# The opening of a one-core decoder layer: dummy products, meta tokens by two transposes, x in halves

## The chip, the core and the metric

The kernel runs on one core of a Trainium2 chip. The metric is the device time of one execution in microseconds (us), and the median of three runs is given. The core has a matrix engine (PE in the profile, with its weight loads as PEld), a vector engine (DVE), a scalar engine (ACT), GpSimd (POOL) and a sync engine (SP). SP, ACT and POOL also issue DMA transfers, each in the order of its own instruction stream.

## What is computed

One layer of a hybrid decoder trunk. 16 learned meta tokens stand ahead of 256 tokens of x, so 272 tokens of width 2048 go through. All values are float32.

```python
h = jnp.concatenate([meta_b, x], axis=1)          # 16 + 256 tokens, 2048 wide
u = rms_norm(h, g_pre_mix)
z_pool, v_conv, g_conv, gate_a, gate_b = jnp.split(u @ w_in, splits, axis=-1)
y_a = causal_multiscale_pool(z_pool, w_pool_grp, pool_scale) @ w_pool_out
y_b = conformer_conv(v_conv, g_conv, w_dw, ...) @ w_conv_out
m = sigmoid(gate_a) * y_a + sigmoid(gate_b) * y_b
h = h + rms_norm(m @ w_o, g_post_mix)
h = h + rms_norm(jnp.square(relu(rms_norm(h, g_pre_mlp) @ w_up)) @ w_down, g_post_mlp)
return h[:, 16:]
```

For this change only the first product counts: the columns `v_conv` of `u @ w_in`, and what has to be there before it can begin.

## The kernel before, in words

**Number format.** Each float32 operand is split into a rounded high part (`hi`, by a copy on ACT) and the rest (`lo`, by a subtraction on DVE). A product of two such operands is three passes on PE: high weight with high activation, high weight with low activation, low weight with high activation (`mm3`, line 417; its matmul is line 422). The activations are transposed so that channels lie on the 128 partitions: `u[:, k, 0, :]` is the high part and `u[:, k, 1, :]` the low part of channel group k (16 groups of 128), the first 16 columns being the meta tokens and the other 256 those of x. The norm's root is left out at first: only its gain `g_pre_mix` is multiplied in, and the root of each token is multiplied into the results later (`scale_roots`, `scale_rows`).

**Loads of the opening** (lines 323 to 334). SP loads `m_in`, the meta tokens as 16 rows of 2048 (128 KB). ACT loads the gain as 16 rows of 128 (`load_rows`, line 300). x comes in four blocks of 512 columns (`load_x`, line 318); block 0 goes as two transfers of 256 KB, one of its two token tiles on SP and one on ACT. `open_chunk` (line 233) begins a chunk of weights: it takes a buffer `raw` and issues its transfers; a chunk of the first stretch has eight row groups of 128 by 256 columns, which come in pieces of 1, 1, 2, 2 and 2 row groups on the queues that the argument `first` lists. x block 1 follows on ACT, block 2 on SP, then the second chunk, then block 3. POOL loads the small vectors and the taps. The transfers of SP and ACT count up eight semaphores in turn; a transfer that takes a semaphore for a second time waits, on the engine that issues it, until the transfer that had it before has landed. `warm_up(AF.Sqrt)` makes ACT load its function table.

**First work on PE.** `keep_warm(n)` (line 341) puts n transposes of the identity into a tile that nobody reads. Eight of them stand first. `meta_tokens` (line 351) then transposes `m_in` in 16 pieces of 16 rows by 128 columns (line 355), turns the gain into columns (`rows_to_columns`, lines 312 and 313), multiplies the two on DVE (`mg`, line 359), and splits the result into the first 16 columns of `u` (lines 360 and 361). Four more dummies follow.

**The first product** (lines 521 to 539). Two accumulators of 128 by 272 take 16 steps k. `x_tile(k)` (line 366) transposes the two token tiles of channel group k on PE (line 370) into a PSUM tile `xt`, from which ACT writes the high part (line 371) and DVE the low part (line 372). `pieces_to(n)` splits the weights' row groups up to n (lines 250 and 253). The loop runs four steps ahead of the product (`LEAD`): for k = -4 to -1 it only makes x tiles 0 to 3 and splits row groups 0 to 4. Then step k of the product is six matmuls of 272 columns, two times the three passes, and after each odd k two more x tiles are made. So x tiles 4 and 5, the first that need x block 1, stand behind the steps 0 and 1. Everything on an engine runs in the order in which it is written here; only later parts of the kernel are ordered by the planner at the top of the file (`Plan`).

Of the kernel before, what the change touches and what calls it, by code (L numbers as in the profile page):

```python
# [8 lines left out]
F32 = mybir.dt.float32  # L9
F32R = mybir.dt.float32r  # L10
AF = mybir.ActivationFunctionType
# [3 lines left out]
P = 128  # L15
CK = 4
CW = 512
# [83 lines left out]
def hybrid_block(ctx: ExitStack, tc: tile.TileContext, ins: dict, out: bass.AP):  # L101
    nc = tc.nc
    x = ins["x"][0]
    meta = ins["meta"]
    T, D = x.shape
    M = meta.shape[0]
    L = M + T
    NT = T // P
    KD = D // P
# [17 lines left out]
    const = ctx.enter_context(tc.tile_pool(name="const", bufs=1))  # L127
# [3 lines left out]
    tmp = ctx.enter_context(tc.tile_pool(name="tmp", bufs=2))  # L131
# [3 lines left out]
    def f32(ap):  # L135
        return ap.bitcast(F32)

    def acc_tile(name):
        return psA.tile([P, CW], F32, tag="acc", name=name)

    def misc_tile(name):
        return psB.tile([P, CW], F32, tag="misc", name=name)
# [43 lines left out]
    HALF = (2 * CK, CW // 2)  # L186
# [24 lines left out]
    opened = []  # L211
# [13 lines left out]
    def part_tile(tag, n, standing=False):  # L225

        key = f"{tag}{n % 3}"
        room = ready.pop(key) if key in ready else part_room(key, f"{tag}_{n}")
        place = 2 if standing and tag == "hi" else 1
        shift = (place - 1 - 3 * KEYS.index(key)) % 4 * LINE  # L230
        return room[:, shift:shift + CK * CW]

    def open_chunk(first=((2, nc.sync),) * 4):
        n = at["n"]
        at["n"] += 1
        src, (rows, width) = stream[n]
        raw = raws.tile([P, CK * CW], F32, tag="raw", name=f"raw_{n}")
        hi, lo = (part_tile(tag, at["parts"], n in standing_chunks) for tag in ("hi", "lo"))
        at["parts"] += 1
        flat, (raw, hi, lo) = raw, (t.rearrange("p (k c) -> p k c", k=rows) for t in (raw, hi, lo))  # L240
        pieces = rows if n < FIRST + 1 else 1
        k = rows // pieces
        i = 0
        for n_, queue in first if n < FIRST else ((rows, nc.sync),):
            sl = slice(i, i + n_)
            queue.dma_start(raw[:, sl, :], src[:, sl, :])
            i += n_

        def high(sl):
            nc.scalar.copy(hi[:, sl, :], raw[:, sl, :])  # L250

        def low(sl):
            nc.vector.tensor_sub(lo[:, sl, :], raw[:, sl, :], f32(hi[:, sl, :]))  # L253

        def piece(i):
            def f():
                sl = slice(i * k, (i + 1) * k)
                high(sl)
                low(sl)
            return f  # L260
        opened.append((hi, lo, [piece(i) for i in range(pieces)], flat))
# [13 lines left out]
        return opened.pop(0)[:2]  # L275


    ident = const.tile([P, P], F32, name="ident")
    make_identity(nc, ident)
    ones = const.tile([P, P], F32, name="ones")  # L280
# [3 lines left out]
    def warm_up(func):  # L284

        nc.scalar.activation(warm, ones[:, 0:1], func)
# [3 lines left out]
    m_in = big.tile([M, D], F32, tag="a", name="m_in")  # L290
# [9 lines left out]
    def load_rows(queue, *names):  # L300
        rows = tmp.tile([48, P], F32, tag="g", name=f"rows_{names[0]}")
        n = 0
        for name in names:
            v = ins[name][0].rearrange("(k p) -> k p", p=P)
            queue.dma_start(rows[n:n + v.shape[0], :], v)
            n += v.shape[0]
        return rows, n, names[0]

    def rows_to_columns(rows, n, name):

        pv = misc_tile(f"pv_{name}")
        nc.tensor.transpose(pv[:, :n], rows[:n, :], ident[:n, :n])
        nc.vector.tensor_copy(vecs[:, cols[name]:cols[name] + n], pv[:, :n])

    def col(name, k):
        return vecs[:, cols[name] + k:cols[name] + k + 1]

    def load_x(queue, b, ts=slice(0, NT)):
        sl = slice(b * CW, (b + 1) * CW)
        queue.dma_start(x_in[:, ts, sl], xv[:, ts, sl])  # L320


    nc.sync.dma_start(m_in, meta)
    pre_rows = load_rows(nc.scalar, "g_pre_mix")
    for t, queue in enumerate((nc.sync, nc.scalar)):
        load_x(queue, 0, slice(t, t + 1))
    open_chunk(((1, nc.scalar), (1, nc.sync), (2, nc.sync), (2, nc.sync), (2, nc.sync)))
    load_x(nc.scalar, 1)
    load_x(nc.sync, 2)
    open_chunk()  # L330
    load_x(nc.sync, 3)
    other_rows = load_rows(nc.gpsimd, "pool_scale", "b_dw", "conv_ln_g", "conv_ln_b", "g_pre_mlp")
    taps_in = big.tile([TAPS, CC], F32, tag="c", name="taps_in")
    nc.gpsimd.dma_start(taps_in, w_dw)
    ssq = const.tile([P, NT + 1, XB], F32, name="ssq")
    nc.gpsimd.memset(ssq, 1.0)
    warm_up(AF.Sqrt)

    idle = misc_tile("idle")

    def keep_warm(n):
        for _ in range(n):
            nc.tensor.transpose(idle[:, :P], ident, ident)

    keep_warm(8)

    u = big.tile([P, KD, 2, -(-L // (4 * LINE)) * 4 * LINE], F32R, tag="um", name="u")[:, :, :, :L]

    def meta_tokens():

        pt = acc_tile("xm")[:, :KD * M].rearrange("p (k m) -> p k m", k=KD)
        for k in range(KD):
            nc.tensor.transpose(pt[:, k, :], m_in[:, k * P:(k + 1) * P], ident[:M, :M])
        rows_to_columns(*pre_rows)
        mg = tmp.tile([P, KD, M], F32, tag="v", bufs=5, name="mg")
        g = vecs[:, cols["g_pre_mix"]:cols["g_pre_mix"] + KD]
        nc.vector.tensor_mul(mg, pt, g[:, :, None].broadcast_to([P, KD, M]))
        nc.scalar.copy(u[:, :, 0, :M], mg)  # L360
        nc.vector.tensor_sub(u[:, :, 1, :M], mg, f32(u[:, :, 0, :M]))

    meta_tokens()
    keep_warm(4)

    def x_tile(k):
        pt = acc_tile(f"xt_{k}")[:, :T]
        sl = slice(k * P, (k + 1) * P)
        for t in range(NT):
            nc.tensor.transpose(pt[:, t * P:(t + 1) * P], x_in[:, t, sl], ident)  # L370
        nc.scalar.activation(u[:, k, 0, M:], pt, AF.Copy, scale=col("g_pre_mix", k))
        nc.vector.scalar_tensor_tensor(
            u[:, k, 1, M:], pt, col("g_pre_mix", k), f32(u[:, k, 0, M:]),
            op0=ALU.mult, op1=ALU.subtract)

    def sq_tile(b, t):
        sl = slice(b * CW, (b + 1) * CW)
        junk = tmp.tile([P, CW], F32, tag="junk", bufs=1, name=f"sqx_{b}_{t}")
        src, n = (x_in[:, t, sl], P) if t < NT else (m_in[:, sl], M)
        nc.scalar.activation(junk[:n, :], src, AF.Square, accum_out=ssq[:n, t, b:b + 1])  # L380
# [6 lines left out]
        nc.vector.tensor_scalar(q, q, -0.5, 1.5, op0=ALU.mult, op1=ALU.add)  # L387
        nc.vector.tensor_mul(r, r, q)

    rb = const.tile([P, L], F32, name="rb")  # L390
    sc = {}

    def scale_roots():
# [23 lines left out]
    def mm3(acc, hi, lo, act, k, cs, first, last):  # L417


        off = act.shape[3] - acc.shape[1]  # L420
        for n, (w, a) in enumerate(((hi, 0), (hi, 1), (lo, 0))):
            nc.tensor.matmul(acc, w[:, k[0], cs], act[:, k[1], a, off:],  # L422
                             start=first and n == 0, stop=last and n == 2)
# [18 lines left out]
    def acc_tiles(name, n=CW // P):  # L442
        return [acc_tile(f"acc_{name}_{j}") for j in range(n)]
# [68 lines left out]
    def pieces_to(n):  # L512

        while first["split"] < min(n, (FIRST + 1) * HALF[0]):
            c = first["split"] // HALF[0]
            if c == at["n"]:
                open_chunk()
            opened[c][2].pop(0)()
            first["split"] += 1

    first = {"split": 0}
    accs = [acc[:, :L] for acc in acc_tiles("v0", HALF_CW // P)]
    squares = [(b, t) for b in range(XB) for t in range(NT + 1)]
    LEAD = 4
    for k in range(-LEAD, KD):
        if k < 0:
            x_tile(k + LEAD)

        pieces_to(min(k + LEAD + 1, KD) + 2 * max(k - KD + LEAD + 1, 0))
        if k < 0:  # L530
            continue
        if k >= HALF[0] and k % 2:
            sq_tile(*squares.pop(0))
        for j, acc in enumerate(accs):
            mm3(acc, *opened[k // HALF[0]][:2], u, (k % HALF[0], k), slice(j * P, (j + 1) * P),
                k == 0, k == KD - 1)
        if k % 2:
            for kx in range(k + LEAD - 1, min(k + LEAD + 1, KD)):
                x_tile(kx)
# [183 lines left out]
    for g in range(NG):  # L723
        for j in range(GK):
            q = g * GK + j
            acc = (acc_tile if q < KP - 2 else misc_tile)(f"acc_grp_{q}")[:, :T]
# [48 lines left out]
    for n in range(NB):  # L775
# [4 lines left out]
    m = big.tile([P, LINE + KD * 2 * T], F32R, tag="um", name="m")[:, LINE:].rearrange(  # L780
        "p (k a t) -> p k a t", k=KD, a=2)
# [421 lines left out]
    accs = acc_tiles("up00")  # L1203
# [498 lines left out]
    for e, cs in enumerate(col_halves):  # L1702
        for w, s in ends:
            h = AT[s][0]
# [47 lines left out]
```

## Time and profile before

| | |
|---|---|
| median of 3 runs | 1208.1 us (1207.75 to 1208.54) |
| the profiled execution's own time | 1208.15 us |
| its span in the profile | 1206.4 us |
| PE busy | 1195.8 us, 99% of the span |
| DVE busy | 974.7 us, 81% |
| ACT busy | 627.6 us, 52% |
| DMA | 238.27 MB, mean 198 GB/s |
| first dummy on PE | 1.35 us after the span's start |
| `m_in` needed and there | 3.87 us |
| first matmul of the first product | 8.26 us |
| x tile 4 on PE | 10.88 us |

Times in a view are microseconds from the start of the span. The profiled execution has 1.75 us outside the span. A row of the timeline is a run of equal instructions that follow one another on one engine: when the first began, how long it took until the last ended, and how many. The chain of waits is followed back from the last instruction of the window to what released it. A row of DMA issues gives the size of a transfer and the time from its issue to the landing of its last part; `ACTq` and `SPq` are the issuing streams of ACT and SP.

### The profile page before, as it was taken

What the parts mean: (1) busy time and instruction counts of PE and PEld (TensorE: products, weight loads), DVE (VectorE), ACT (ScalarE), POOL (GpSimd) and SP (SyncE); (2) the same over time, 40 slices, a digit from 0 to 9 for tenths busy, and PEclk for the clock granted to TensorE, in tenths of its full rate; (3) what the DMA queues carried; (4) which work ended last, traced back from release to release, by engine and by line L of the source; (5) the groups of instructions that cost most, each with busy time, mean ns of one, the idle gap of its engine ahead of it and who ended that gap; (6) DMA issues with size and microseconds to landing.
All of it is one profiled execution on the core that took longest, in us unless ns stands there. A gap on an engine that the chain in (4) does not pass through costs nothing.

```text
span 1206.4 us, 15712 instructions
## 1 busy us (share of the span) xinstructions
PE 1195.8 (99%) x6444; PEld 1038.4 (86%) x6444; DVE 974.7 (81%) x1058; ACT 627.6 (52%) x651; POOL 8.3 (1%) x19
## 2 busy tenths in 40 slices
PE   9999999999999999999999999999999999999997
PEld 9999988888888888898888888888888888888886
DVE  6799978999776778688988878778878778888756
ACT  7533344443583454665555564564554555555542
POOL 1000000000000000000000000000000000000000
PEclk9999999999999999999999999999999999999999
DMA  9655555656558578546475674674764764755841
GB/s 289 210 175 175 178 202 180 208 177 207 175 169 280 176 256 262 181 160 221 144 244 174 187 232 158 198 249 141 245 199 156 261 200 149 244 175 178 275 141 70
DMA packets 162038, 238.27 MB, mean 198 GB/s; under 512 B 4033, under 2 KB 91521, under 8 KB 161440
## 3 DMA queue, kind: packets, MB, share of 16 engines
q1 hardware_dynamic: 159120, 229.98, 58.2%
q0 software_dynamic: 1680, 5.40, 1.7%
q10 hardware_dynamic: 1168, 1.91, 0.4%
q8 instruction: 50, 0.82, 0.3%
q14 instruction: 20, 0.16, 0.0%
HBM read 235.17 MB, written 2.10 MB: 197 GB/s over the span
## 4 chain that ended last, share of the span: by engine, by line
PE 99%; DVE 0%; DMA 0%; DVEq 0%; ACT 0%; issue 0%; ACTq 0%
PE bank_u L427 18%; PE acc_gate L682 14%; PE acc_up L1516 14%; PE bank_u L433 9%; PE bank_a L1516 7%; PE o_c L1020 6%; PE bank_b L1516 5%; PE acc_v L422 4%; PE acc_z L422 4%; PE acc_g L422 4%; PE acc_co L682 4%; PE acc_po L682 4%; PE acc_up L427 1%; PE bank_u L1516 1%; PE o_a L1020 1%; PE acc_up L433 1%
## 5 line engine op out<-in xcount | busy, mean ns | idle before, releaser
L427 PE MATMUL bank_u<-m,hi 128*128 128x512 f32 x960 | 329.9, 390 | 0.0
L433 PE MATMUL bank_u<-m,lo 128*128 128x256 f32 x960 | 265.5, 277 | 0.0
L250 ACT CAST hi<-raw 128x2048 fp32r<-128x2048 f32 (+1 forms) x99 | 151.7, 1548 | 188.9 <-PE acc_gate L682 71.5
L1367 DVE TENSOR_TENSOR lo<-raw_m,hi 128x2048 fp32r<-128x2048 f32 x85 | 194.4, 2289 | 59.2 <-ACT hi L1362 59.2
L1362 ACT CAST hi<-raw_m 128x2048 fp32r<-128x2048 f32 x85 | 162.5, 1912 | 138.1 <-PE bank_u L427 76.8
L253 DVE TENSOR_TENSOR lo<-raw,hi 128x2048 fp32r<-128x2048 f32 (+1 forms) x99 | 180.6, 1835 | 44.1 <-ACT hi L250 43.8
L427 PEld LDWEIGHTS bank_u<-m,hi 128*128 128x128 f32 x960 | 180.2, 188 | 37.9
L433 PEld LDWEIGHTS bank_u<-m,lo 128*128 128x128 f32 x960 | 180.3, 188 | 1.6
L682 PE MATMUL acc_gate<-hi,u 128*128 128x512 f32 x512 | 158.6, 390 | 0.0
L1516 PE MATMUL acc_up<-hi,forms 128*128 128x512 f32 x496 | 157.5, 389 | 0.0
L488 DVE SCALAR_TENSOR_TENSOR c<-a,taps,c 128x256 f32<-128x256 f32 x240 | 115.5, 484 | 7.1 <-ACT c L482 0.5
L682 PEld LDWEIGHTS acc_gate<-hi,u 128*128 128x128 f32 x512 | 96.1, 188 | 20.0
L1516 PEld LDWEIGHTS acc_up<-hi,forms 128*128 128x128 f32 x496 | 93.1, 188 | 19.5
L682 PE MATMUL acc_gate<-lo,u 128*128 128x512 f32 x256 | 99.6, 389 | 0.0
L1516 PE MATMUL acc_up<-lo,forms 128*128 128x512 f32 x248 | 96.6, 389 | 0.0
L1367 DVE TENSOR_TENSOR lo<-raw_c,hi 128x2048 fp32r<-128x2048 f32 x29 | 66.4, 2290 | 21.0 <-ACT hi L1362 21.0
L1516 PE MATMUL bank_a<-hi,forms 128*128 128x512 f32 (+1 forms) x256 | 82.0, 383 | 0.0
L1362 ACT CAST hi<-raw_c 128x2048 fp32r<-128x2048 f32 x29 | 55.3, 1908 | 51.1 <-PE bank_u L427 28.1
L1367 DVE TENSOR_TENSOR lo<-raw_a,hi 128x2048 fp32r<-128x2048 f32 x29 | 66.4, 2289 | 18.4 <-ACT hi L1362 18.4
L1362 ACT CAST hi<-raw_a 128x2048 fp32r<-128x2048 f32 x29 | 55.4, 1910 | 42.4 <-PE bank_u L427 17.1
L1020 PE MATMUL o_c<-hi,m 128*128 128x512 f32 x208 | 65.6, 390 | 0.0
L1516 PE MATMUL bank_b<-hi,forms 128*128 128x512 f32 (+1 forms) x200 | 63.7, 382 | 0.0
(303 smaller groups left out, 1857.1 us busy)
## 6 DMA issues: line engine op xcount, KB each, us to landing
raw<-in_w_in_dram SPq DMA_DIRECT2D x54, 1024.0 KB, 5.1
raw_m<-in_w_down_dram SPq DMA_DIRECT2D x37, 1024.0 KB, 5.3
raw_m<-in_w_up_dram SPq DMA_DIRECT2D x33, 1024.0 KB, 6.2
raw_c<-in_w_down_dram SPq DMA_DIRECT2D x14, 1024.0 KB, 5.3
raw_a<-in_w_up_dram SPq DMA_DIRECT2D x13, 1024.0 KB, 6.0
raw_a<-in_w_down_dram SPq DMA_DIRECT2D x13, 1024.0 KB, 5.2
raw_c<-in_w_up_dram SPq DMA_DIRECT2D x12, 1024.0 KB, 6.0
raw_o<-in_w_o_dram SPq DMA_DIRECT2D x10, 1024.0 KB, 7.5
```

The source lines that it names most:

```text
L250: nc.scalar.copy(hi[:, sl, :], raw[:, sl, :])
L253: nc.vector.tensor_sub(lo[:, sl, :], raw[:, sl, :], f32(hi[:, sl, :]))
L422: nc.tensor.matmul(acc, w[:, k[0], cs], act[:, k[1], a, off:], start=first and n == 0, stop=last and n == 2)
L427: nc.tensor.matmul(acc.rearrange("p (a t) -> p a t", a=2)[:, :, ts], hi[:, k[0], cs], act[:, k[1], :, off + ts.start:off + ts.stop], start ...
L433: nc.tensor.matmul(acc[:, :T], lo[:, k[0], cs], act[:, k[1], 0, off:], start=False, stop=stop, skip_group_check=True)
L488: nc.vector.scalar_tensor_tensor(c, conv["a"][:, q, i:i + T], taps[:, q, i:i + 1], c, op0=ALU.mult, op1=ALU.add)
L682: nc.tensor.matmul(acc, act(kk)[:, a_, ts_], w_[:, k, :], start=kk == 0 and n == 0, stop=kk == nk - 1 and n == 2)
L1020: nc.tensor.matmul(acc, form(k, a_), box[w_][:, k, :], start=start and k == 0 and n == 0, stop=stop and k == CK - 1 and n == 2, skip_group ...
L1362: nc.scalar.copy(box["flat"], raw)
L1367: nc.vector.tensor_sub(lo, raw, f32(box["flat"]))
L1516: nc.tensor.matmul(acc, forms[h][:, f, k, a_, :], box[w_][:, k, cs], start=start and k == 0 and n == 0, stop=stop and k == KH - 1 and n == ...
```

## The change

- `rb`, a tile of 128 by 272 that existed already for a later use, is allocated first, and its first 128 columns are set to 1.0 by DVE. The dummies of `keep_warm` are now float32 products of these columns with themselves, not transposes of the identity. Eight stand first as before; the four behind the meta tokens are gone; one stands ahead of step 0 of the product.
- The meta tokens are loaded a first time as `m_rows`, 256 rows of 128 numbers on 128 partitions (256 pieces of 512 bytes, 128 KB in all), and transposed by two transposes of 128 by 128. The 16 rows `m_in` are loaded later, behind the second weight chunk; they are still needed for the sum of squares.
- x block 0 comes as four transfers of 128 KB: for each token tile the first 256 columns ahead of the weights, and the other 256 after the first weight piece.
- `warm_up(AF.Sqrt)` moves ahead of the load of x block 1, which ACT issues.
- The meta tokens' split (cast on ACT, subtraction on DVE) moves behind x tile 0.
- Step 0 of the first product is issued behind x tile 1 instead of behind x tile 3. The order of all later instructions is the same on each engine.

```diff
         for n_, queue in first if n < FIRST else ((rows, nc.sync),):
+            if n_ == 0:
+                queue()
+                continue
...
+    rb = const.tile([P, L], F32, name="rb")
+    nc.vector.memset(rb[:, :P], 1.0)
...
-    def load_x(queue, b, ts=slice(0, NT)):
-        sl = slice(b * CW, (b + 1) * CW)
+    def load_x(queue, b, ts=slice(0, NT), cs=(0, 2)):
+        sl = slice(b * CW + cs[0] * CW // 2, b * CW + cs[1] * CW // 2)
         queue.dma_start(x_in[:, ts, sl], xv[:, ts, sl])
...
-    nc.sync.dma_start(m_in, meta)
+    m_rows = tmp.tile([P, M * KD // P, P], F32, tag="v", bufs=5, name="m_rows")
+    nc.sync.dma_start(m_rows, meta.rearrange("m (k f) -> (m k) f", f=P).rearrange(
+        "(h p) f -> p h f", p=P))
     pre_rows = load_rows(nc.scalar, "g_pre_mix")
-    for t, queue in enumerate((nc.sync, nc.scalar)):
-        load_x(queue, 0, slice(t, t + 1))
-    open_chunk(((1, nc.scalar), (1, nc.sync), (2, nc.sync), (2, nc.sync), (2, nc.sync)))
+    load_x(nc.sync, 0, slice(0, 1), (0, 1))
+    load_x(nc.scalar, 0, slice(1, 2), (0, 1))
+
+    def rest_of_block():
+        load_x(nc.sync, 0, slice(0, 1), (1, 2))
+        load_x(nc.scalar, 0, slice(1, 2), (1, 2))
+    open_chunk(((1, nc.scalar), (0, rest_of_block), (1, nc.sync), (2, nc.sync), (2, nc.sync),
+                (2, nc.sync)))
+    warm_up(AF.Sqrt)
     load_x(nc.scalar, 1)
     load_x(nc.sync, 2)
     open_chunk()
+    nc.sync.dma_start(m_in, meta)
     load_x(nc.sync, 3)
...
-    warm_up(AF.Sqrt)
...
-            nc.tensor.transpose(idle[:, :P], ident, ident)
+            nc.tensor.matmul(idle[:, :P], rb[:, :P], rb[:, :P], start=True, stop=True)
...
-        pt = acc_tile("xm")[:, :KD * M].rearrange("p (k m) -> p k m", k=KD)
-        for k in range(KD):
-            nc.tensor.transpose(pt[:, k, :], m_in[:, k * P:(k + 1) * P], ident[:M, :M])
+        pt = acc_tile("xm")[:, :KD * M]
+        for h in range(KD * M // P):
+            nc.tensor.transpose(pt[:, h * P:(h + 1) * P], m_rows[:, h, :], ident)
+        pt = pt.rearrange("p (m k) -> p k m", k=KD)
...
+        return mg
+
+    mg = meta_tokens()
+
+    def split_meta():
         nc.scalar.copy(u[:, :, 0, :M], mg)
         nc.vector.tensor_sub(u[:, :, 1, :M], mg, f32(u[:, :, 0, :M]))
-
-    meta_tokens()
-    keep_warm(4)
...
+    def product_of(k):
+        for j, acc in enumerate(accs):
+            mm3(acc, *opened[k // HALF[0]][:2], u, (k % HALF[0], k), slice(j * P, (j + 1) * P),
+                k == 0, k == KD - 1)
+
     for k in range(-LEAD, KD):
         if k < 0:
             x_tile(k + LEAD)
+        if k == -LEAD:
+            split_meta()
         pieces_to(min(k + LEAD + 1, KD) + 2 * max(k - KD + LEAD + 1, 0))
+        if k == 1 - LEAD:
+            keep_warm(1)
+            product_of(0)
         if k < 0:
             continue
         if k >= HALF[0] and k % 2:
             sq_tile(*squares.pop(0))
-        for j, acc in enumerate(accs):
-            mm3(acc, *opened[k // HALF[0]][:2], u, (k % HALF[0], k), slice(j * P, (j + 1) * P),
-                k == 0, k == KD - 1)
+        if k:
+            product_of(k)
```

More of the change, by code (lines that the diff above doesn't have):

```diff
@@ L388, in rsqrt @@
         nc.vector.tensor_mul(r, r, q)
-    rb = const.tile([P, L], F32, name="rb")
     sc = {}
```

## The prediction

> **What bounds the kernel now.** I read the page first, for the shares of the span and of the chain that ended last.
>
> ```profile
> PE 1195.8 (99%) x6444; PEld 1038.4 (86%) x6444; DVE 974.7 (81%) x1058; ACT 627.6 (52%) x651; POOL 8.3 (1%) x19
> ...
> PE 99%; DVE 0%; DMA 0%; DVEq 0%; ACT 0%; issue 0%; ACTq 0%
> ```
>
> PE is the chain nearly from end to end. So a microsecond gained or lost before PE runs without a gap moves the end by the same microsecond, and the whole question is when that point comes. Next the same chain, of the first 15 us alone, in order of time (start, duration, what).
>
> ```profile
> 0.74 3.08 DMA m_in<-in_meta_dram
> ...
> 3.87 1.89 PE xm L355 x16
> ...
> 5.86 1.05 PE idle L343 x4
> 6.91 1.71 PE xt L370 x8
> 8.61 2.43 PE acc_v L422 x12
> 11.04 0.44 PE xt L370 x4
> 11.48 1.49 PE acc_v L422 x12
> ```
>
> Two things are to be seen. The twelve products of steps 0 and 1 take 2.43 us and the next twelve 1.49 us: the first run at a slow clock. (The granted clock of the windows view shows 1.00 there, since it has no record before the first change; the spacing of the products is what shows it.) And from 11.04 on, x tiles and products follow each other, 1.93 us for two steps. I use the start of x tile 4 as the mark: whatever happens ahead, from there PE has work. The timeline puts it at 10.88, with the steps before it:
>
> ```profile
> 0.73 0.42 ACTq L305 DMA_DIRECT2D rows_g_pre_mix<-in_g_pre_mix_dram  x1
> ...
> 1.19 0.44 ACTq L320 DMA_DIRECT2D x_in<-in_x_dram  x1
> ...
> 1.35 1.97 PE L343 MATMUL idle<-ident 128*128 128x128 f32 x8 [1.35 <-POOL ident masks.py:199]
> ...
> 7.37 0.47 ACT L371 ACTIVATE u<-xt,vecs 128x256 fp32r<-128x256 f32 x1 [0.40 <-PE xt L370]
> ...
> 7.74 0.39 ACT L250 CAST hi<-raw 128x256 fp32r<-128x256 f32 x1
> ...
> 8.04 0.48 ACT L371 ACTIVATE u<-xt,vecs 128x256 fp32r<-128x256 f32 x1
> ...
> 8.26 0.80 PE L422 MATMUL acc_v<-u,hi 128*128 128x272 f32 x2
> 8.28 0.42 DVE L253 TENSOR_TENSOR lo<-raw,hi 128x256 fp32r<-128x256 f32 x1
> ...
> 8.86 0.48 PE L422 MATMUL acc_v<-u,lo 128*128 128x272 f32 x1
> ...
> 10.88 0.60 PE L370 MATMUL xt<-ident,x_in 128*128 128x128 f32 x4
> ```
>
> Step 0 begins at 8.26, 0.13 us after the first weight cast ends (7.74 + 0.39 = 8.13). ACT is the gate: its operations here follow each other every 0.30 to 0.37 us. The product pays 2.62 us from 8.26 to 10.88; at the later spacing twelve products take 1.49.
>
> Last the transfers: what moved in each microsecond (last column GB/s), and single transfers with their size and time to landing.
>
> ```profile
> 1.00:2.00 1.00, 0.65 (x3) 1.00 0.52 123
> 2.00:3.00 1.00, 1.00 (x7) 1.00 0.74 125
> 3.00:4.00 1.00, 0.46 (x4) 1.00 0.87 197
> 4.00:5.00 1.00, 1.00 (x11) 1.00 0.86 274
> 5.00:6.00 1.00, 1.00 (x10) 1.00 1.02 346
> 6.00:7.00 1.00, 1.00 (x6) 1.00 1.08 398
> ```
>
> ```profile
> m_in<-in_meta_dram SPq DMA_DIRECT2D x1, 128.0 KB, 3.1
> rows_g_pre_mix<-in_g_pre_mix_dram ACTq DMA_DIRECT2D x1, 8.0 KB, 3.3
> x_in<-in_x_dram ACTq DMA_DIRECT2D x1, 256.0 KB, 5.1
> raw<-in_w_in_dram SPq DMA_DIRECT2D x1, 256.0 KB, 6.8
> x_in<-in_x_dram ACTq DMA_DIRECT2D x1, 512.0 KB, 8.1
> raw<-in_w_in_dram SPq DMA_DIRECT2D x1, 256.0 KB, 4.0
> x_in<-in_x_dram SPq DMA_DIRECT2D x1, 512.0 KB, 6.4
> ```
>
> The issues of two of them, from the timeline:
>
> ```profile
> 2.12 0.44 SPq L246 DMA_DIRECT2D raw<-in_w_in_dram  x1
> ```
>
> ```profile
> 2.14 0.46 ACTq L320 DMA_DIRECT2D x_in<-in_x_dram  x1
> ```
>
> The x transfer of 512 KB on ACT is block 1: issued at 2.14, landed at 10.24, used at 10.88. It has 0.64 us to spare. The first 256 KB weight row is the piece with row groups 2 and 3, issued at 2.12 and landed at 8.9; the second, with 4.0 us, is a later piece, issued when the queues were running.
>
> **The change part by part.** *Dummies.* They no longer wait for the identity on POOL. DVE's memset isn't in the trace. The first engines start at 0.73 and the dummies now at 1.35, so they begin between these; I take 0.95. A float32 product is two recorded passes, and at full clock passes follow each other like transposes:
>
> ```profile
> L1405 PE MATMUL bank_b<-diag,ones x4: 270/274/275, 555.7 to 556.0; 128*128 128x128 f32 x4
> ```
>
> Four in 0.3 us, 0.11 apiece, and four transposes at 10.88 likewise ((0.60 - 0.27) / 3 = 0.11). At the slow clock the eight transposes at 1.35 stand 0.22 apart, so a dummy costs 0.43 and eight 3.4 us, to about 4.4. They are over by the time x arrives, and cost the path nothing. What they may buy is the clock: real products in a row from 0.95 to 4.4. Before, 28 transposes up to 6.9 (8, 16 and 4) didn't raise it: step 0 still began slow, and it rose only while its products and those of step 1 ran. I take it as up by step 0. That is worth up to 2.62 - 1.49 = 1.1 us on steps 0 and 1, if nothing else holds them.
>
> *Meta tokens.* Two transposes replace sixteen (1.89 us) and the four dummies (1.05). `m_rows` lands between `m_in`'s 3.1 us after issue and the 5.1 of 256 KB, so by 3.9 to 5.8; I take 4.4, near the row of the same bytes. The transposes, the gain's copy and the product `mg` follow within about a microsecond and are hidden under the wait of ACT below; if that wait were gone, they would be ready by 5.7. The second load of `m_in` is 128 KB on SP behind the second chunk and is read only by sums of squares behind the x tiles; nothing early waits for it.
>
> *x in halves.* Bytes needed for x tiles 0 and 1: 128 + 8 + 256 KB = 0.40 MB. The windows reach that at 3.8. Landing trails the mean: block 0 before needed 0.66 MB, reached at 4.8, and landed at 6.3 (ACT's half, 1.19 + 5.1), so 1.5 us. Hence 5.3, against 6.3 before. One microsecond gained, by this part alone.
>
> *The moved table load, and what it moves.* This is where I part from the intention. The built program shows, for ACT and for SP:
>
> ```
> 7 L326 DMACopy x_in<-in_x_dram 128x2x512 [waits DMAHW0_49]
> 4 L249 DMACopy raw_104<-in_w_in_dram 128x2x256 [waits DMAHW0_49]
> ```
>
> Eight semaphores serve the transfers in turn. Before, x block 1 was the fifth and waited for nothing. Now two more transfers are on the queues and block 1 stands behind the table load; by then its semaphore has been taken by the gain rows and again by the weight piece with row groups 2 and 3. So ACT stops at the issue of x block 1 until that weight piece has landed. Behind it on ACT stand x tile 0, the meta cast, the first weight cast and all later ones. The trace has the same thing on SP, whose issue of a weight piece waited for x block 1:
>
> ```profile
> SPq L246 <- DMA x_in<-in_x_dram: 2.5, 1, 2.5
> ```
>
> SP issues the piece once the gain rows have landed, at 4.0 (0.73 + 3.3). Ahead of it are 128 + 8 + 512 + 256 KB, with it 1160 KB = 1.19 MB. The windows sum to 1.07 MB at 6.0, the rest takes 0.12 / 0.398 = 0.31: 6.3. With the lag of 1.5 us it lands at 7.8. The ends: the bytes alone, 6.3; as late as before, 8.9.
>
> From 7.8: one issue, 0.46, so ACT starts x tile 0 at 8.26 (before 7.37). One operation more, the meta cast, stands ahead of the first weight cast, which begins at 8.26 + 0.37 + 0.33 = 8.96 and ends 0.39 later, at 9.35. Step 0 begins at 9.5, 1.2 us later than before. The low weights follow at 9.5 to 9.95 (0.42); the last four products then end at 9.95 + 4 x 0.124 = 10.45. x tiles 2 and 3 take 0.44, step 1 six products, 0.75: 11.65.
>
> Then x tile 4 needs x block 1, issued at 7.8 rather than 2.14. Its landing has no row of its own: 3.1 us is what 128 KB took into empty queues, 6.4 what 512 KB took behind a full one. I take 4.4, nearest to the 4.0 that 256 KB took in running queues, since it has ACT's queue to itself but shares the engines with SP's pieces: 12.2. So x tile 4 begins near 12.25, against 10.88. Casts for steps 2 to 5 are done by then, so PE runs on as before. The loss is 12.25 - 10.88 = 1.4 us.
>
> *Sum.* Of the profiled execution, 1208.15 + 1.4 = 1209.5. That execution lies 0.05 above the median of 1208.1, which I leave out. Step 0 ahead of x tiles 2 and 3 costs nothing here: PE waits for x block 1 anyway. Without that cover ACT would wait for x tile 2 some 0.5 us longer, as PE transposes it behind step 0.
>
> **Rivals.** *Short wait.* The weight piece lands at 6.7, between the bytes alone and my value. Then step 0 begins at 8.35, step 1 ends at 10.55, and x block 1, with 3.8 us of flight (between 3.1 and my 4.4), is there at 10.5. x tile 4 at 10.6: 0.3 gained, 1207.9. For it speaks that bytes alone allow it; against it, that every landing in the rows trails the mean by over a microsecond.
>
> *No such wait on the path, the change works as meant.* x halves at 5.3, ACT starts at 5.75, first weight cast 6.5 to 6.9, step 0 at 7.0. Its low weights end at 7.5, so it ends at 8.0; x tiles 2 and 3 to 8.4; step 1 to 9.15. Now ACT must do x tiles 2 and 3 and two casts after 8.1, DVE follows, and step 3's low weights come at 10.1; steps 2 and 3 end at 11.1 instead of 12.97. That gives 1206.3. It would need the wait to be over by 5.3, which no row of bytes allows.
>
> *Slow clock again, the case on the slower side.* PE stands idle from about 5.9, when x tiles 0 and 1 (5.3 + 4 x 0.11) and the lone dummy are done, until 9.5. The end of the run shows what idling does:
>
> ```profile
> 1197.00:1198.00 1.00, 0.67 (x6) 0.46 (x4) 0.75 (x2) 0.00 (x0) 0.00 (x0) 1.00 0.31 109
> ...
> 1201.00:1202.00 1.00, 0.00 (x0) 0.00 (x0) 1.00 (x2) 0.00 (x0) 0.00 (x0) 0.86 0.47 177
> 1202.00:1203.00 1.00, 0.00 (x0) 0.00 (x0) 0.89 (x3) 0.00 (x0) 0.00 (x0) 0.50 0.73 281
> ```
>
> PE's last product ends at 1197.67, and the granted clock falls to 0.50 at 1201.72 (0.86 is 72% at 1.00): 4.05 us of idling. My gap is 3.6 us, so this decides from a gap half a microsecond longer, or if the lone dummy doesn't count. Then the last four products of step 0 take 0.9 from 9.95, four transposes 0.9, step 1 1.36: 13.1 instead of 12.25, and the next transposes 0.4 more. Loss 2.6, 1210.8. [...]
>
> **How the numbers follow.** 0.2% of 1208.1 is 2.4 us, about what a measurement of this kernel can tell from no change. Forecast 0.52: 1209.5, its own range 1208.6 to 1210.4 by the landing of the weight piece half a microsecond either way and of x block 1. Short wait 0.15: 1207.9. As meant 0.08: 1206.3. Slow clock 0.20: 1210.8. A remaining 0.05 is x block 1 landing at 6.4 us after issue, 14.2, with 1211.5. The range 1207.4 to 1211.1 leaves out the case as meant and the tail of the last. Faster by over 0.2% (below 1205.7) needs more than I can find: 0.03. Slower by over 0.2% (above 1210.5): most of the slow clock and the remainder, 0.24. Within: 0.73.
>
> **What would show it.** Right: an ACT queue row in which the issue of x block 1 waits for a weight transfer, ending between 7 and 8.5 us; the first x tile on ACT after 8; x tile 4 on PE released by x block 1 near 12; products of step 0 about 0.124 apart. Wrong: ACT's first x tile before 7.4 (then the wait is short or not there), products 0.23 apart at 9.5 to 13 (slow clock), or PE gaps after 13 us, which I hold for excluded because the later order is the same on every engine.

## The result, and the profile after

The changed kernel takes 1215.74 us (median of 6 runs, 1214.51 to 1217.35) against 1208.09 us for the kernel before (6 runs, 1207.75 to 1208.68). The ratio is 1.0063, 95% interval 1.005 to 1.0076: 7.65 us slower. The profiled execution took 1217.35 us, with a span of 1215.4 us, 9.0 us more than before. It is the slowest of the six, 1.6 us above their median, so the pieces below add up to its 9.0 us and not to 7.65.

The chain of waits of the changed kernel over its first 34 us (start, duration, what):

```profile
0.73 2.06 DMA rows_g_pre_mix<-in_g_pre_mix_dram
...
2.81 5.20 DMA raw<-in_w_in_dram
...
8.04 8.53 DMA x_in<-in_x_dram
...
16.71 1.09 PE xt L388 x4
17.80 2.72 PE acc_v L439 x12
20.52 0.85 PE xt L388 x4
21.37 2.03 PE acc_v L439 x12
23.40 0.44 PE xt L388 x4
23.84 1.49 PE acc_v L439 x12
```

Three transfers in a row lead to x tile 4: the gain rows, the weight piece that SP issues once they have landed, and x block 1, which ACT issues once that piece has landed. Its flight of 8.53 us is the longest piece. x tile 4 starts at 16.71, against 10.88 before: 5.83 us later. Behind it two pairs of steps run at the slow spacing (2.72 and 2.03 us, with transposes of 1.09 and 0.85) ahead of the first at the usual 0.44 and 1.49: another 0.65 + 1.23 + 0.41 + 0.54 = 2.83 us. That is 8.66 of the 9.0 us; 0.3 us I do not assign.

The timeline shows the same on the engines (in brackets the idle time before, and who ended it):

```profile
2.71 1.28 ACT L291 ACT_TABLE_LOAD   x1 [2.71 <-issue]
...
8.04 0.47 ACTq L326 DMA_DIRECT2D x_in<-in_x_dram  x1
8.62 0.47 ACT L389 ACTIVATE u<-xt,vecs 128x256 fp32r<-128x256 f32 x1 [4.42 <-DMA raw<-in_w_in_dram]
```

```profile
1.05 3.79 PE L358 MATMUL idle<-rb 128*128 128x128 f32 x16 [1.05 <-DVE rb L282]
...
5.41 0.66 PE L388 MATMUL xt<-ident,x_in 128*128 128x128 f32 x4
5.90 0.39 PE L358 MATMUL idle<-rb 128*128 128x128 f32 x2
9.75 0.84 PE L439 MATMUL acc_v<-u,hi 128*128 128x272 f32 x2 [3.46 <-ACT hi L253]
...
16.71 1.09 PE L388 MATMUL xt<-ident,x_in 128*128 128x128 f32 x4 [2.88 <-DMA x_in<-in_x_dram]
```

PE is idle twice, 3.46 us before step 0 and 2.88 us before x tile 4. Until 5.9 everything runs as early as the change means it to: x tiles 0 and 1 at 5.41 instead of 6.70.

Why did x block 1 fly for 8.53 us? The DMA queues of the changed kernel, packets, MB and share of 16 engines, in four stretches (8 to 10, 11 to 12, 12 to 13 and 13 to 14 us). q1 carries what SP issues; q10 what ACT issues (0.93 MB on q10 in the first 24 us, the 904 KB of ACT's five transfers):

```profile
q1 hardware_dynamic: 397, 0.58, 98.1%
...
q1 hardware_dynamic: 371, 0.36, 110.6%
...
q1 hardware_dynamic: 199, 0.19, 58.3%
q10 hardware_dynamic: 85, 0.17, 50.0%
...
q10 hardware_dynamic: 117, 0.24, 70.5%
q1 hardware_dynamic: 114, 0.12, 35.7%
```

From 8 to 12 us there is no row for q10 (nor from 10 to 11, which is not shown): ACT's transfer, issued at 8.04, moves nothing for four microseconds, while SP's fill the engines (0.58 MB in the first two microseconds, 0.36 in the last). From 12 on the two queues share: 85 packets of q10 beside 199 of q1 up to 13 us, then 117 beside 114. Where ACT's transfer waited until then, no run here shows.

What it waited for can be estimated. Ahead of 8.04 SP had issued eleven transfers, 2560 KB or 2.62 MB, and q1 had moved 1.13 MB by 8 us. So about 1.5 MB was issued and not yet moved, and 1.3 MB of it moved before ACT's first packet: x block 1 came when what SP had issued before it was nearly through. In before_early_table, below, the same estimate gives 1.4 MB outstanding and 1.2 MB moved first.

The last view is the windows, cut so that the two changes of the granted clock, 13.65 us apart, fall on cuts with four equal pieces of 3.41 us between them (start and end, length, PE busy, granted clock; the last two columns are the DMA engines' share and GB/s):

```profile
5.37:8.79 3.42, 0.92 (x7) 1.00 1.05 313
8.79:12.20 3.41, 2.45 (x11) 0.50 1.06 344
...
19.03:22.44 3.41, 3.41 (x17) 0.50 0.89 282
22.44:25.85 3.41, 3.41 (x30) 1.00 0.48 161
```

The clock was full ahead of 8.79 (the four transposes from 5.41 stand (0.66 - 0.27) / 3 = 0.13 us apart). It fell there, when PE had been idle for 2.50 us (since 5.90 + 0.39 = 6.29), and came back only at 22.44, 13.65 us later. PE was busy throughout the last of the four pieces between, and for 2.45, 1.62 and 2.32 us in the three ahead of it.

### The profile page after: what moved, and what is told of

Its sections match the earlier page's. It is cut to its first block, busy times and chain, and to the rows that moved or that the text cites. A ratio compares the mean times of both kernels' runs of the same rounds, so it can differ in the third digit from the quotient of the medians.

```text
span 1215.4 us, 15704 instructions
## 1 busy us (share of the span) xinstructions
PE 1198.8 (99%) x6436; PEld 1041.1 (86%) x6436; DVE 974.9 (80%) x1059; ACT 628.4 (52%) x651; POOL 8.3 (1%) x19
## 4 chain that ended last, share of the span: by engine, by line
PE 98%; DMA 1%; DVE 0%; DVEq 0%; ACT 0%; issue 0%; ACTq 0%
PE bank_u L444 18%; PE acc_gate L709 14%; PE acc_up L1543 14%; PE bank_u L450 9%; PE bank_a L1543 7%; PE o_c L1047 6%; PE bank_b L1543 5%; PE acc_v L439 4%; PE acc_z L439 4%; PE acc_g L439 4%; PE acc_co L709 4%; PE acc_po L709 4%; PE acc_up L444 1%; PE bank_u L1543 1%; DMA x_in<-in_x_dram 1%; PE o_a L1047 1%
```

## The experiments

Four theories stand against each other. **S**: ACT's stop makes x block 1 late, and this is the loss. **C**: the clock lost in the idle gaps is the loss. **D**: the transfers, more of them and in smaller pieces, put off everything behind them. **O**: step 0 in its new place costs time. A row of the table compares a kernel with runs of the kernel before on the same chip.

| kernel | median us (runs) | before, same chip | difference | ratio, 95% interval |
|---|---|---|---|---|
| changed kernel | 1215.74 (6) | 1208.09 | +7.65 | 1.005 to 1.0076 |
| late_table | 1210.35 (11) | 1208.36 | +1.99 | 1.0007 to 1.0025 |
| before_early_table | 1214.34 (4) | 1208.36 | +5.98 | 1.0036 to 1.0064 |
| b1_on_sp | 1210.91 (10) | 1208.36 | +2.55 | 1.0013 to 1.0031 |
| fill | 1213.72 (4) | 1208.36 | +5.36 | 1.0033 to 1.0061 |
| late_whole | 1210.71 (11) | 1208.12 | +2.59 | 1.0011 to 1.0028 |
| late_old_order | 1210.97 (11) | 1208.12 | +2.85 | 1.0014 to 1.0032 |
| late_transposes | 1211.35 (8) | 1208.12 | +3.23 | 1.0015 to 1.0036 |
| before_float | 1209.24 (11) | 1208.12 | +1.12 | 1.0 to 1.0017 |
| before_two_loads | 1208.53 (11) | 1208.09 | +0.44 | 0.9995 to 1.0013 |
| one_load | 1209.07 (11) | 1208.09 | +0.98 | 1.0002 to 1.0019 |
| held | 1210.26 (11) | 1208.09 | +2.17 | 1.0009 to 1.0027 |
| one_load_held | 1208.72 (11) | 1208.09 | +0.63 | 0.9998 to 1.0016 |

An interval is about 1 us wide to either side, and 1.6 to 1.7 us in the rows of 4 and 6 runs. So differences of about a microsecond between two rows are not told apart.

### The late issue of x block 1

**late_table**, the changed kernel with the table load behind the issue:

```diff
-    warm_up(AF.Sqrt)
     load_x(nc.scalar, 1)
+    warm_up(AF.Sqrt)
```

> The changed kernel with one line moved: ACT issues x block 1 ahead of its table load again. In the built program that transfer then waits only for the gain rows (2.8 us in the changed kernel's trace) and not for weight row groups 2 and 3 (8.0 us). Theory S (the wait on ACT, and the late issue of x block 1 behind everything that SP has issued by then): ACT's first x tile begins before 6.5 us instead of 8.6, x tile 4 before 10.5 instead of 16.7, and the time falls from 1215.7 to 1206.3, at most 1207.5. Rival C (the clock: eight float32 dummies raise it early, an idle PE loses it, and that alone costs most): PE still idles between the dummies and step 0, the clock still falls, and the time stays above 1211. Rival D (256 pieces of 512 bytes and the x halves slow all transfers of the opening): x tile 4 gets no earlier than the 10.9 of before, and the time is 1208 or more.

Measured +1.99 us in place of +7.65: not the 1206.3 of S, and not over 1211 as C has it. D's bound on the time holds, but not its reason: x tile 4 is earlier than 10.9. The timeline shows the issue of x block 1 (the second of the two in the row of ACT) over at 3.20, and x tile 4 at 10.18, ahead of the 10.88 before the change:

```profile
2.22 0.98 ACTq L326 DMA_DIRECT2D x_in<-in_x_dram  x2
...
10.53 0.41 ACT L253 CAST hi<-raw 128x256 fp32r<-128x256 f32 x1 [1.68 <-DMA raw<-in_w_in_dram]
```

```profile
6.90 0.51 PE L439 MATMUL acc_v<-u,hi 128*128 128x272 f32 x2 [0.87 <-ACT hi L253]
...
10.18 0.63 PE L388 MATMUL xt<-ident,x_in 128*128 128x128 f32 x4 [0.87 <-DMA x_in<-in_x_dram]
...
12.82 0.60 PE L388 MATMUL xt<-ident,x_in 128*128 128x128 f32 x4
...
19.67 0.63 PE L388 MATMUL xt<-ident,x_in 128*128 128x128 f32 x4 [0.89 <-DMA x_in<-in_x_dram]
```

So S carries some 5.7 us of the 7.65. But the change still doesn't pay. The 0.70 us won at x tile 4 is gone at x tile 6 (12.82, against 12.80 before): ACT had waited 1.68 us for a weight piece, and its cast at 10.53 comes late. At x tile 12 PE waits 0.89 us for x block 3 and stands 1.09 us behind the kernel before (19.67 against 18.58).

**before_early_table**, the converse: the kernel before with only this line moved.

```diff
+    warm_up(AF.Sqrt)
     load_x(nc.scalar, 1)
 ...
-    warm_up(AF.Sqrt)
```

> The kernel before with this one line of the change alone: the table load stands ahead of the issue of x block 1 on ACT. Dummies, meta tokens and x block 0 are those of before. In the built program x block 1 then waits for the first weight row group (7.3 us in the trace of before). Theory S: x block 1 is issued near 7.4, ACT's first x tile begins at 7.8 instead of 7.4, x block 1 lands behind the 0.6 MB that SP has outstanding by then, near 12.3, x tile 4 begins there instead of at 10.9, and the time is 1209.5 to 1211. Rivals C and D: neither the dummies nor the transfers' pieces have changed, so 1208.1 within 0.3.

Measured +5.98: more than either expected. Timeline and chain:

```profile
2.15 1.28 ACT L286 ACT_TABLE_LOAD   x1 [2.15 <-issue]
...
6.97 0.46 ACTq L320 DMA_DIRECT2D x_in<-in_x_dram  x1
7.47 0.41 ACT L360 CAST u<-mg 128x256 fp32r<-128x256 f32 x1 [3.82 <-DMA raw<-in_w_in_dram]
...
14.46 1.01 PE L370 MATMUL xt<-ident,x_in 128*128 128x128 f32 x4 [2.88 <-DMA x_in<-in_x_dram]
```

```profile
6.97 7.34 DMA x_in<-in_x_dram
...
15.46 2.69 PE acc_v L422 x12
18.15 0.44 PE xt L370 x4
```

One moved line reproduces both parts: ACT held until a weight piece lands, a flight of 7.34 us, PE idle for 2.88 us, and then slow products. The other edits aren't needed for most of the loss: 5.98 of 7.65 us, with intervals that overlap.

**b1_on_sp**, the changed kernel with x block 1 issued by SP:

```diff
-    load_x(nc.scalar, 1)
+    load_x(nc.sync, 1)
```

> The changed kernel, but SP issues x block 1, ahead of x block 2, and the table load keeps its early place. ACT then waits for no transfer issue. Theory S: x block 1 is issued near 5.0 and lands where x block 2 landed in the changed kernel, at 11.5; step 0 begins near 7.0, x tile 4 near 11.5 instead of 16.7; the time is 1208 to 1210, better by some 6 us than the changed kernel and not as good as with x block 1 issued at 2.8. Rival C: the clock falls as in the changed kernel, above 1211. Rival D: as for theory S or later.

Measured +2.55, 0.9 us above the expected times; but ACT's stop is gone here too, and with it 5.1 us. What is left of the wait stands in the timeline:

```profile
11.70 0.63 PE L388 MATMUL xt<-ident,x_in 128*128 128x128 f32 x4 [1.90 <-DMA x_in<-in_x_dram]
```

**fill**, the changed kernel with dummies in both idle gaps, so that PE is not idle there:

```diff
-            keep_warm(1)
+            keep_warm(16)
 ...
+                if kx == LEAD:
+                    keep_warm(18)
                 x_tile(kx)
```

> The changed kernel with more dummies in its two idle stretches on PE: 16 instead of 1 ahead of step 0, and 18 ahead of x tile 4. The wait on ACT stays. This holds the clock and nothing else. Theory S: x tile 4 still begins at 16.5 to 17, the products behind it stand 0.124 us apart from the start and not 0.227, and the time is 1213.5 to 1214.5: the wait is 5.8 us of the loss and the slow clock behind it the other 2 to 3. Rival C: with the clock up the loss is mostly gone, 1210 or less. Rival D says nothing of this run.

Measured +5.36, as S has it. x block 1 is issued at 8.24 and lands 7.9 us later, at about 16.1; x tile 4 begins at 16.32, right behind the last dummies, which cover that landing by less than 0.1 us. It is as late as S says, but the clock is full:

```profile
16.32 0.63 PE L388 MATMUL xt<-ident,x_in 128*128 128x128 f32 x4
16.70 0.50 PE L439 MATMUL acc_v<-u,hi 128*128 128x272 f32 x2
```

So the lost clock is worth 7.65 - 5.36 = 2.3 us, near the 2.83 that the chain gave, and the late transfer the rest. The size is rough, since the intervals of the two rows overlap; their runs don't (1213.34 to 1214.12 us against 1214.51 to 1217.35, on two chips). With late_table, S and C stand as cause and consequence: without the late issue PE's longest gap between its first dummy and x tile 12 is 0.89 us.

### What is left without the late issue

**late_whole**, late_table with x block 0 in two whole transfers:

```diff
-    load_x(nc.sync, 0, slice(0, 1), (0, 1))
-    load_x(nc.scalar, 0, slice(1, 2), (0, 1))
+    load_x(nc.sync, 0, slice(0, 1))
+    load_x(nc.scalar, 0, slice(1, 2))
 
     def rest_of_block():
-        load_x(nc.sync, 0, slice(0, 1), (1, 2))
-        load_x(nc.scalar, 0, slice(1, 2), (1, 2))
+        pass
```

> The kernel late_table (changed kernel, table load behind the issue of x block 1; 1210.35 us) with x block 0 in two whole transfers of 256 KB again instead of four halves. Theory D (the front is paced by its transfers, and the halves put the whole row of later ones back: the sixth weight issue's middle packet landed at 9.35 us instead of 7.71, x block 2's at 12.74 instead of 11.65): about 1.1 us less, 1209.2 us (1208.7 to 1209.7). Theory O (step 0 between x tiles 1 and 2 holds the engine) and theory C (the clock) see no reason for a change: 1210.0 to 1210.7 us, or more by the later start of x tiles 0 and 1.

+2.59: the halves aren't what costs; D fails in this term. Two things are in its profile. The clock fell and rose again, which the windows show as means over a microsecond (0.74 is 0.48 us at full and 0.52 at half, so it fell at 7.48; 0.55 puts the rise at 10.90, 3.42 us later):

```profile
7.00:8.00 1.00, 0.28 (x2) 0.74 1.07 388
10.00:11.00 1.00, 1.00 (x7) 0.55 1.07 356
```

And late in the opening PE waits again, far behind the edits. Chain and waits:

```profile
21.57 7.01 DMA raw<-in_w_in_dram
...
29.02 1.91 ACT hi L253
```

```profile
PE pb L428 <- DVE diag L422: 0.7, 1, 0.7
```

A 1 MB weight piece lands at 28.59; ACT's cast of it and the squares queued behind the cast come late, and with them the norm's root (`diag`) that PE needs at 43.27.

**late_old_order**, late_table with step 0 back behind x tile 3:

```diff
-            product_of(0)
 ...
-        if k:
-            product_of(k)
+        product_of(k)
```

> late_table with step 0 back behind x tile 3, as before the change; all else as in late_table. Theory O: the last 2 us against the kernel before come from step 0 waiting ahead of x tiles 2 and 3; 1208.1 to 1209.0 us. Theory D: the second halves of x block 0 land at 10.05 us whatever stands ahead of them on PE, and the same transfers follow; 1210.0 to 1211.5 us, above late_table if step 0 no longer fills that gap.

+2.85, within the times of D: O falls; step 0's new place costs nothing that can be measured.

**late_transposes**, late_table with transposes of the identity as dummies:

```diff
-            nc.tensor.matmul(idle[:, :P], rb[:, :P], rb[:, :P], start=True, stop=True)
+            nc.tensor.transpose(idle[:, :P], ident, ident)
```

> late_table with its eight dummy products as transposes of the identity again, so that the clock should rise only with the first real products. Theory C: the clock comes up some 4 to 6 us later, steps 0 and 1 run at half speed; 1211.5 to 1212.5 us. Theory D: PE waits for transfers in four places of the first 20 us anyway and the slower products fit in those waits; 1210.0 to 1211.0 us.

+3.23, between the two expectations and 1.2 us above late_table: the dummies may be worth a microsecond there, but the intervals overlap. Inconclusive.

**before_float**, the kernel before with float32 dummies alone:

```diff
-            nc.tensor.transpose(idle[:, :P], ident, ident)
+            nc.tensor.matmul(idle[:, :P], rb[:, :P], rb[:, :P], start=True, stop=True)
```

> The kernel before with one part of the change alone: its 8 and 4 dummy transposes become float32 products of a tile of ones set ahead of the identity. Theory C alone: the clock is full from some 5 to 7 us on instead of 10.47, worth half of 3.5 to 5 us less about 0.8 us of longer dummies; 1206.2 to 1207.3 us. Theory D: x block 1 landed 0.84 us and x block 3 0.6 us ahead of the transposes that read them, so no more than 0.6 us can be won before PE waits for a transfer; 1207.4 to 1208.2 us.

+1.12, a miss for both, on the slower side. The timeline tells why: the dummies take twice as long, eight of them push `xm` from 3.87 to 4.77, the other four the x tiles from 6.70 to 8.56 and step 0 from 8.26 to 10.12. Nor did the clock rise at 5 to 7 us: the eight transposes from 8.56 still stand (1.87 - 0.27) / 7 = 0.23 us apart, and the products are the first at full speed. x tile 4 begins at 11.95, 1.07 us later than before.

```profile
4.77 1.88 PE L357 MATMUL xm<-ident,m_in 16*128 16x16 f32 x16
...
6.69 2.08 PE L345 MATMUL idle<-rb 128*128 128x128 f32 x8
8.56 1.87 PE L372 MATMUL xt<-ident,x_in 128*128 128x128 f32 x8
10.12 0.56 PE L423 MATMUL acc_v<-u,hi 128*128 128x272 f32 x2
```

**before_two_loads**, the kernel before with a second load of the meta tokens, into a tile that nothing reads:

```diff
+    nc.sync.dma_start(m_rows, meta.rearrange("m (k f) -> (m k) f", f=P).rearrange(
+        "(h p) f -> p h f", p=P))
     load_x(nc.sync, 3)
```

> The kernel before with one part of the change alone: the meta tokens are loaded a second time, into a tile that nothing reads, on SP behind the second weight chunk and ahead of x block 3 (128 KB more). Theory D (the front is paced by its transfers): every later landing of the first 30 us is 0.4 to 0.8 us later; x block 3 had 0.6 us to spare and the big weight pieces behind it feed ACT's squares, so 1208.3 to 1209.0 us, with the weight piece that landed at 26.93 us landing at 27.4 to 27.8. Theory C (clock alone makes the remaining loss): 1208.1 us and no difference.

+0.44, as D has it, though the interval holds zero. The profile shows the wait that the kernel before doesn't have, and the 1 MB piece that lands at 27.50 (20.68 + 6.82, against 26.93 before) behind it. In this execution PE was ahead (x tile 4 at 10.42, 0.46 us earlier than before), and that lead ends in the wait:

```profile
PE pb L415 <- DVE diag L409: 0.4, 1, 0.4
```

```profile
20.68 6.82 DMA raw<-in_w_in_dram
```

**one_load**, late_whole with the meta tokens loaded once and transposed from `m_in` as before:

```diff
-    nc.sync.dma_start(m_rows, meta.rearrange("m (k f) -> (m k) f", f=P).rearrange(
-        "(h p) f -> p h f", p=P))
+    nc.sync.dma_start(m_in, meta)
 ...
-    nc.sync.dma_start(m_in, meta)
 ...
-        for h in range(KD * M // P):
-            nc.tensor.transpose(pt[:, h * P:(h + 1) * P], m_rows[:, h, :], ident)
+        for k in range(KD):
+            nc.tensor.transpose(pt[:, k, :], m_in[:, k * P:(k + 1) * P], ident[:M, :M])
```

> late_whole (table load late, x block 0 whole; 1210.71 us) with the meta tokens loaded once and transposed by 16 products from that tile, as before the change. Theory D: the weight piece that ended late_whole's chain at 28.59 us lands 0.4 to 0.8 us earlier and the last product with it; 1209.8 to 1210.3 us, the 0.68 us idle ahead of the scale's products gone or under 0.3. Theory C: the meta tokens come 1 us later and take 16 transposes; 1210.7 to 1211.5 us.

+0.98 against late_whole's +2.59: 1.6 us, more than D's 0.4 to 0.8, though the intervals of the two rows overlap. Behind the first dummy PE waits only 0.3 us ahead of step 0 in the first 60 us; the 0.7 us for `diag` is gone, and the 1 MB piece takes 5.1 us in place of late_whole's 7.01. The runs fall into two groups, seven from 1208.58 to 1209.09 us and four from 1209.82 to 1210.27; the profiled one, 1209.9, is of the upper. There the timeline has step 0 at 8.54, at the slow clock (0.85 us for its first two products, as in the changed kernel), and x tile 4 at 12.42:

```profile
4.77 1.89 PE L366 MATMUL xm<-ident,m_in 16*128 16x16 f32 x16
...
8.54 0.85 PE L434 MATMUL acc_v<-u,hi 128*128 128x272 f32 x2 [0.31 <-ACT hi L253]
...
12.42 0.73 PE L383 MATMUL xt<-ident,x_in 128*128 128x128 f32 x4
```

So x tile 4 is 1.54 us later than in the kernel before, and the distance hardly grows: 1.70 us at the last x tiles (22.21 against 20.51) and at the products of `diag` (43.47 against 41.77). All that this execution loses is lost in the opening, on PE, and not to a transfer.

**held**, late_whole with four dummies behind the meta tokens and four ahead of step 0:

```diff
     mg = meta_tokens()
+    keep_warm(4)
 ...
-            keep_warm(1)
+            keep_warm(4)
```

> late_whole with four dummy products after the meta tokens and four instead of one ahead of step 0, so that PE is not idle before x tile 4. In late_whole's profile the clock fell at 7.48 us and rose again at 10.90. Theory C: steps 0 and 1 at full clock, about 1 us less; 1209.3 to 1209.9 us. Theory D: what ends late is the weight piece at 28.6 us and ACT's squares behind it, which no clock moves; 1210.3 to 1211.2 us.

+2.17, just below D's times and above C's. It is 0.42 us below late_whole, which the intervals don't tell from nothing: what a held clock saves here, the dummies that hold it may cost again.

**one_load_held**, one_load with 6 dummies first, one behind the meta tokens and four ahead of step 0 (counts as in held's diff):

> The version the runs point to: late_whole with the meta tokens loaded once, six dummies at the start, one behind the meta tokens and four ahead of step 0. Theories D and C together: landings as in the kernel before, clock up by step 0 or 1, x tile 4 as soon as x block 1 lands at some 10.2 us (0.7 us ahead of before); 1207.4 to 1208.3 us. If another queue effect or the fixed chain of squares sets the end, it stays at 1208.5 to 1210 us.

+0.63, above the hoped-for 1207.4 to 1208.3, and not to be told from the kernel before. From held to one_load_held, on the same chip, it is 1.5 us (1209.55 to 1212.79 against 1208.29 to 1209.76); besides the second load, some dummies are gone there and the meta tokens' transposes are the sixteen of before, so the step isn't the load's alone. Behind its first dummy PE waits for nothing in the first 60 us. x tile 4 is again late, by 0.77 us, and the distance stays (0.81 at 42.58, the products of `diag`):

```profile
11.65 0.60 PE L384 MATMUL xt<-ident,x_in 128*128 128x128 f32 x4
```

No version here is faster than the kernel before.

## Why the prediction was wrong, point by point

- **The mechanism**: right. ACT stops at the issue of x block 1 until the weight piece lands, and the issue comes at 8.04, 0.02 us after that landing, as SP's issue of the piece came at 2.81, 0.02 us after that of the gain rows. late_table and before_early_table show that this one wait makes most of the loss (5.7 of 7.65 us when it alone is taken out, 5.98 when it alone is put in).
- **Dummies, meta tokens, x halves**: dummies from 1.05 to 4.84 (forecast 0.95 to 4.4); meta tokens and halves earlier than forecast, x tiles 0 and 1 at 5.41. Hidden under ACT's wait, as forecast.
- **The wait and what follows on ACT**: right. The piece landed at 8.02 (forecast 7.8), ACT's x tile 0 began at 8.62 (8.26), step 0 at 9.75 (9.5). That 7.8 came so near is in part luck: the gain rows landed at 2.79 and not 4.0, so SP issued the piece 1.2 us earlier, and it then flew 5.20 us instead of 3.8.
- **x block 1's flight**: the step that failed. The prediction says "Its landing has no row of its own" and takes 4.4 us, "since it has ACT's queue to itself". It took 8.53, and 7.34 in before_early_table. The row was there: the same 512 KB on ACT had taken 8.1 us in the profile of before, quoted in the same part. The 4.0 us chosen instead belonged to a transfer of half the size on another queue, and a queue of one's own was no help: ACT's transfer moved nothing until 12 us. With the 8.1 of that row the landing would have been put at 15.9 and x tile 4 about 5.1 us late instead of 1.4. x tile 4 began at 16.71 and not at 12.25; 4.1 of these 4.5 us are this one term. The remainder case, with 6.4 us and a chance of 0.05, was the nearest to it and still too short.
- **Slow clock again**: it came true beside the forecast, not in place of it. As a rival with a chance of 0.20 it was no part of the sum of 1209.5. It was priced for one gap of 3.6 us and 1.2 us more; there were two gaps, and with the late transfer the slow stretch lasted until 22.44. fill puts it at 2.3 us.
- **How long PE may idle**: the rival took its limit from one reading, the 4.05 us of idling at the end of the run, and counted a gap of 3.6 us as half a microsecond short of it. The opening shows no such limit. At the fall at 8.79 PE had been idle for 2.50 us, and busy for 0.92 of the 3.42 us before. In late_whole the clock fell at 7.48 with PE idle for 0.39 us, and in before_early_table at 14.56 (a mean of 0.78 from 14 to 15 us), 0.10 us after a gap of 2.88 us had ended. So the rival's chance was put too low. Nor was the time to the rise always the same: 13.65 us in the changed kernel, 3.42 in late_whole and in before_early_table (up at 17.98, by a mean of 0.51 from 17 to 18 us).
- **The second load of `m_in`**: "nothing early waits for it" was true and missed the point. What stands behind it on SP is later: the 1 MB piece that SP issues at 20.7 to 22.8 us takes 6.1 to 7.7 us in the seven profiles with two loads and no late issue, and 5.1 to 5.8 in the four with one. What that is worth in time is less sure: taking the load out gained 1.6 and 1.5 us, with the transposes changed too and, in the second case, the dummies, and adding it to the kernel before cost 0.44, which the interval doesn't tell from nothing.
- **"As meant", 1206.3**: with the stop removed x tile 4 did come earlier (10.18), yet late_table ran at 1210.35. The prediction held PE gaps after 13 us for excluded because the order of the instructions is the same there; late_table has them at 19.67 and, as a wait for `diag` of 0.6 us, at 44.07. The order was the same, the landings were not.

What remains open: one_load and one_load_held are still 1.0 and 0.6 us above the kernel before, about what their intervals allow. In their profiles the distance is there by x tile 4 (12.42 and 11.65 against 10.88), in dummies, transposes and slow products on PE and not in a landing. How much of it is the dummies' own time and how much the moment at which the clock rises, the runs don't show.

## What to carry to other kernels

Before an instruction is moved ahead of a DMA issue, list what that issue will wait for at its new place, and take the flight of the very same transfer from its own row, at the load it will meet, rather than from a smaller one on another queue. Look at what a second load of the same bytes does to what is queued behind it: here the opening kept the DMA engines full (a share of 1.05 to 1.08 from 5.37 to 19.03 us in the changed kernel), and the 1 MB piece behind a second 128 KB took 6.8 us in before_two_loads, against 5.8 in the kernel before. An earlier first product was worth only what the later landings left of it: in late_table 0.70 us was gone two x tiles later. A gap on PE had two prices, its own length (2.88 us ahead of x tile 4) and the slow products after it (2.83 us by the chain, 2.3 by fill); price both together.

## What the runs showed of the hardware that was not expected

- A transfer that ACT issued at 8.04 us moved its first packet at about 12.2, with 0.58 MB of SP's going ahead from 8 to 10 us alone, though from 13 to 14 us, once both run, the two queues move 117 and 114 packets.
- The clock fell though PE had been busy for 0.92 of the last 3.42 us, and in late_whole though it had been busy for 1.80 of the last 3.41 us, transposes among them:

```profile
4.07:7.48 3.41, 1.80 (x13) 1.00 1.01 341
```

In b1_on_sp it stayed up over a stretch of that length with 1.99 us busy, at the gap ahead of x tile 4 (the four transposes behind the gap stand (0.63 - 0.27) / 3 = 0.12 us apart):

```profile
10.28:13.69 3.41, 1.99 (x17) 1.00 1.07 367
```

- Eight float32 dummies did not settle the clock. With the two wide transposes behind them step 0 of late_table ran at full speed (0.51 us for its first two products); with sixteen narrow ones, as in one_load, the first two still took 0.85. What decides the rise, the runs don't show.
